# A fixed instruction order for the state-space stage of a hybrid decoder layer, with decays prepared in mid-step, the causal select in GpSimd's order, and the decay product last in a step

## The chip, the cores and the metric

The kernel runs on one core of a Trainium2 chip. The metric is the device time of one execution in microseconds (us); lower is better. The core has five engines with a queue of instructions each, which run in the order of the queue and wait for each other through semaphores: TensorE (PE, matrix products and transposes; PEld is its weight load), VectorE (DVE), ScalarE (ACT), GpSimd (POOL) and SyncE (SP). Transfers between DRAM and the core's memory are issued by SP and ACT. Matrix products are accumulated in eight PSUM banks of 128 x 512 float32.

## The reference, cut to what matters

One layer of a hybrid block on a sequence of 1024 tokens and width 1024, all in float32. Two branches read the same modulated input: a chunked gMLP (y_a) and a Mamba-2 state-space branch (y_b); a gate merges them and a last projection follows. The part that is changed here is the state-space scan and the norm behind it: 8 groups of 4 heads of 64 columns, a state of 128, chunks of 128 tokens. `segsum_exp` gives exp(a_cs[i] - a_cs[j]) where i >= j, and 0 elsewhere.

```python
def ssd_scan(x, dt, a, bmat, cmat):
    xd = (x * dt[..., None]).reshape(b, nc, q, g, r, p)
    a_cs = jnp.cumsum(adt, axis=-1)
    decay = segsum_exp(adt)
    cb = jnp.einsum('bclgn,bcsgn->bcgls', cc, bc)
    y_diag = jnp.einsum('bcgls,bcgrls,bcsgrp->bclgrp', cb, decay, xd)
    decay_to_end = jnp.exp(a_cs[..., -1:] - a_cs)
    chunk_states = jnp.einsum('bcsgn,bcgrs,bcsgrp->bcgrpn', bc, decay_to_end, xd)
    ...
    def step(state, inp):
        cs, cd = inp
        return state * cd[..., None, None] + cs, state
    ...
    y_off = jnp.einsum('bclgn,bcgrpn,bcgrl->bclgrp', cc, prev_states, jnp.exp(a_cs))
    return (y_diag + y_off)
...
y_b = y_b + xh * d_skip[:, None]
yz = (y_b * silu(ssm_z)).reshape(b, s, SSM_GROUPS, -1)
y_b = rms_norm(yz, ssm_norm_w.reshape(SSM_GROUPS, -1)).reshape(b, s, SSM_D_INNER)
merged = sigmoid(g_a) * (y_a @ w_proj_a) + sigmoid(g_b) * (y_b @ w_proj_b)
```

## The kernel before

**Stages.** The input is normed and transposed and the first products run (to about 70 us); `v_block` makes the v columns of the input projection by a seven-product scheme (p1 to p7) on halves of the matrix, each operand split into a high and a low part; pairs of columns of the other projections follow (`pair`), to about 920 us; then comes the state-space stage, then the projection of y_b, and the output product to the end.

**The state-space stage** is a list of 32 steps, `order`: two groups take turns, four steps each, and a step covers 256 tokens, two chunks. A step n consists of pieces that the loop at the end of the stage calls:

- `fetch`: SP loads the decay sums of a step, broadcast to all partitions (`dcy`, 512 KB), and the six rows of the step (`sl`, 768 KB: C, B, two of x, two of the gate z). There are five sets of these buffers, so a load into a set waits for the step five earlier.
- `decay`: ScalarE takes exp into `ea` (two instructions, L1067), GpSimd sets what is above the diagonal to -1e30 (`affine_select` on `dcy`, L1070), ScalarE takes eight exponentials of `dcy` in place (L1075).
- `prep`: TensorE makes C times B (`pc`) and transposes x (`px`) and B (the other half of `pc`); VectorE makes `xd` and `xe` from `px` (L1091) and multiplies `dcy` by `pc` (L1095); ScalarE copies B to `bn` (L1097).
- `front`: TensorE makes `yi` from `dcy` and `xd`, and the new states `sp` from `bn` and `xe`; the state is carried over each of the two chunks by a GpSimd product with the chunk's decay (L1123) and a VectorE sum with `sp` (L1125), or copied where there is none yet (L1121).
- `back`: TensorE makes `yn` from the states before the two chunks; `evacuate` adds the skip term to `yi` (L1151), multiplies `yn` by `ea` (`ym`, L1155), adds (L1156) and gates (L1157) on GpSimd; `post` stores every second step's rows (`yb_d`).
- Later pieces (`later(k, ...)`, run after k more pieces): `squares` (two ScalarE squares in place, L1176, and their sum on GpSimd, L1177), `post2` (a row sum by eight `pq` products, a VectorE instruction, L1186, and for each group a power of -0.5 on GpSimd, L1190), `post3` (a transpose, a copy and a store).

Between `front` and `back` of a step, `draw` issues four or five items of the gMLP projection (`proj_a`, tiles `pma`: two matmuls an item), so that TensorE has work while the state is summed. Beside it go the split of its weights (`wa_block`, L1280 and L1281) and the gate of its result (`tha`, L1382), 16 of each.

**What sets the order.** TensorE's instructions and SP's loads are pinned. `pin` (`keep_in_program_order`) puts an instruction behind the one that was traced before it on its engine, whether that one is pinned or not. All other instructions of VectorE, ScalarE and GpSimd are placed in their queue by a planner, which walks through the program by its own estimate of times and takes, of the instructions that it holds to be ready, the one of the highest priority: the earlier in the program, the higher, and those under `tc.high_priority()` (`front`, `back`, `prep`) first. Once placed, an engine's order is fixed. In the kernel before, nearly all of the stage's work on these three engines is left to the planner:

```python
for n in range(len(order)):
    if n > 1:
        step(n, "front")
        draw(6 if n == 2 else 4 + n % 2)
    step(n, "back")
    ...
    if n + 2 < len(order):
        step(n + 2, "prep")
    fetch(n + 6)
    decays(n + 4)
```

`decays(n + 4)` at the end of step n calls `decay` for step n+3.

## Time and profile before

| what | value |
|---|---|
| time, median of 3 runs (lowest to highest) | 1404.81 us (1404.6 to 1406.76) |
| the profiled execution's own time | 1402.83 us |
| its span, first to last instruction | 1401.1 us |
| mean granted TensorE clock | 0.996 |
| DMA traffic | 288.6 MB, mean 206 GB/s |

The page of the profile gives the busy time of each engine and its share of the span. Views of the trace follow in the prediction: busy time by stretches of the span (its columns are the stretch, its length, then for PE, PEld, DVE, ACT and POOL the busy us and the number of instructions, then the granted clock, the DMA share and GB/s); groups of instructions (line, engine, operation, out<-in, shapes, count, then busy us and mean ns of one, then the idle time of the engine before them with what ended it); waits (engine and line, what it waited for: us in total, times, longest); the timeline (start, length, engine, line, operation, in brackets the idle time before it); and the chain of waits that ended last.

### The profile page before, as it was taken

To read this page: it belongs to the slowest core of one execution; us is meant where nothing else is said; L and a number is where in the kernel's file an instruction comes from. 1 tells how busy PE (TensorE), PEld (TensorE's weight loads), DVE (VectorE), ACT (ScalarE), POOL (GpSimd) and SP (SyncE) were. 2 spreads that over 40 slices of the span, in tenths; PEclk is the share of its full clock that TensorE was granted. 3 is DMA by queue.
4 is the path that set the end of the run, shared out by engine and by line. 5 is a ranking of instruction groups with operands and counts; after the bars stand their busy time and mean duration, and the time that the engine had idled before them with its cause. 6 is when DMAs were issued, how large, how long until landed. Compare 5 with 4: busy or idle time off the path is not lost.

```text
span 1401.1 us, 20579 instructions
## 1 busy us (share of the span) xinstructions
PE 1369.7 (98%) x6971; PEld 1135.3 (81%) x6971; DVE 1055.3 (75%) x1815; ACT 804.7 (57%) x1496; POOL 217.8 (16%) x208
## 2 busy tenths in 40 slices
PE   8999999999999999999999999999999999999997
PEld 7678888888888888878888888888888788888786
DVE  4776776687777889888888795398777655859976
ACT  5754656666666566455675555677676623223453
POOL 0000000000000011211000110038878750000001
PEclk9999999999999999999999999999999999999999
DMA  8775433333434777777775774598887658878913
GB/s 263 197 237 147 120 121 120 105 123 118 135 105 128 225 219 230 220 238 226 215 220 148 241 214 134 179 354 319 279 267 278 220 185 280 319 254 313 378 44 120
DMA packets 277181, 288.62 MB, mean 206 GB/s; under 512 B 15788, under 2 KB 224084, under 8 KB 277076
## 3 DMA queue, kind: packets, MB, share of 16 engines
q1 hardware_dynamic: 182420, 203.76, 45.6%
q10 hardware_dynamic: 94656, 83.54, 18.1%
q8 instruction: 55, 0.90, 0.3%
q14 instruction: 50, 0.41, 0.1%
HBM read 199.79 MB, written 87.46 MB: 205 GB/s over the span
## 4 chain that ended last, share of the span: by engine, by line
PE 78%; DVE 7%; DMA 7%; ACT 3%; issue 3%; POOL 2%; SPq 1%; ACTq 0%; DVEq 0%; POOLq 0%
PE xuz L536 6%; PE xx L536 6%; PE xcb L536 6%; PE xz L536 5%; PE xg L536 5%; PE pma L81 4%; PE yx L536 3%; PE vx L918 3%; PE x L1552 3%; PE yuz L536 3%; PE yp L1552 3%; PE ycb L536 3%; PE yz L536 3%; PE ox L1745 2%; PE yg L536 2%
## 5 line engine op out<-in xcount | busy, mean ns | idle before, releaser
L759 POOL TENSOR_TENSOR wog<-wog,gb 128x256 f32<-128x256 f32 x16 | 21.5, 1362 | 624.0 <-DMA wog<-in_w_out_dram 602.9
L1075 ACT ACTIVATE dcy<-dcy,nacs 128x128 f32<-128x128 f32 x256 | 78.7, 388 | 17.2 <-POOL dcy L1070 16.1
L1070 POOL TENSOR_SCALAR_AFFINE_SELECT dcy<-dcy 128x1024 f32<-128x1024 f32 x32 | 35.0, 1094 | 135.4 <-DMA yl<-ya_d 88.7
L990 ACT ACTIVATE ac<-ac 128x1024 f32<-128x1024 f32 x32 | 33.9, 1060 | 25.8 <-DVE ac L988 22.6
L1067 ACT ACTIVATE ea<-dcy 64x512 f32<-64x512 f32 x64 | 40.0, 626 | 12.2 <-DMA dcy<-acs_d 11.8
L81 PE MATMUL pma<-yh,wah 128*128 128x512 f32 x128 | 43.8, 423 | 0.0
L81 PE MATMUL pma<-yh,wal 128*128 128x512 f32 x128 | 43.2, 419 | 0.0
L1490 DVE SCALAR_TENSOR_TENSOR yn<-yn,par,rb 128x512 f32<-128x512 f32 x32 | 23.9, 747 | 24.8 <-DMA yn<-yb_d 24.8
L1155 DVE TENSOR_TENSOR ym<-yn,ea 128x512 f32<-128x512 f32 (+1 forms) x32 | 19.9, 622 | 29.9 <-PE yn L81 29.7
L1095 DVE TENSOR_TENSOR dcy<-dcy,pc 128x1024 f32<-128x1024 f32 x32 | 38.9, 1217 | 3.8 <-PE pc L84 2.6
L1157 POOL TENSOR_TENSOR yz<-y,sl 128x512 f32<-128x512 f32 x32 | 41.4, 1294 | 1.1
L81 PE MATMUL pma<-yl,wah 128*128 128x512 f32 x128 | 40.3, 396 | 0.0
L1156 POOL TENSOR_TENSOR y<-y,ym 128x512 f32<-128x512 f32 (+1 forms) x32 | 36.6, 1143 | 14.5 <-DVE ym L1155 14.5
L81 PE MATMUL yi<-dcy,xd 128*64 128x128 f32 x512 | 35.9, 284 | 2.9 <-DVE st L1125 2.9
L81 PEld LDWEIGHTS yn<-sl,st 128*128 128x128 f32 x224 | 30.3, 190 | 8.8 <-issue 2.7
L81 PE MATMUL yn<-sl,st 128*128 128x128 f32 x224 | 31.4, 276 | 5.4 <-DVE st L1125 5.4
L81 PE MATMUL sp<-xe,bn 128*128 128x256 f32 x112 | 33.6, 418 | 2.9 <-DVE ssq L1186 1.7
L988 DVE SCALAR_TENSOR_TENSOR ac<-c2x,cwt,ac 128x1023 f32<-128x1023 f32 (+2 forms) x24 | 31.2, 1298 | 5.7 <-ACT ac L986 5.6
L1760 POOL TENSOR_TENSOR r<-r,fnw 128x512 f32<-128x512 f32 x2 | 2.5, 1296 | 208.2 <-ACT junk L1758 208.2
L988 DVE SCALAR_TENSOR_TENSOR ac<-c2cb,cwt,ac 128x1023 f32<-128x1023 f32 (+2 forms) x24 | 31.1, 1294 | 4.8 <-ACT ac L986 4.7
L1123 POOL TENSOR_TENSOR st<-st,cd 128x256 f32<-128x256 f32 x48 | 32.5, 677 | 11.2 <-PE yn L81 7.1
L952 ACT ACTIVATE vm<-vm,vr 128x128 f32<-128x128 f32 x64 | 25.8, 483 | 14.0 <-DMA vm<-v_d 13.5
(2903 smaller groups left out, 4421.7 us busy)
## 6 DMA issues: line engine op xcount, KB each, us to landing
sl<-s_d SPq DMA_DIRECT2D x32, 768.0 KB
s_d<-ac ACTq DMA_DIRECT2D x32, 512.0 KB
dcy<-acs_d SPq DMA_DIRECT2D x32, 512.0 KB
av<-in_w_in_dram SPq DMA_DIRECT2D x36, 256.0 KB
aw<-in_ada_w_dram SPq DMA_DIRECT2D x16, 512.0 KB
wbr<-in_w_proj_b_dram SPq DMA_DIRECT2D x64, 128.0 KB
wb_d<-wbb ACTq DMA_DIRECT2D x32, 256.0 KB
wb_d<-wbc ACTq DMA_DIRECT2D x32, 256.0 KB
```

What stands on the lines that cost most here:

```text
L81: pin(PE.matmul(acc, l, r, start=first, stop=last))
L536: pin(PE.matmul(ps, lw[:, k * P : (k + 1) * P], r[k], start=first and n + k == 0, stop=n == 2 and k == 3, skip_group_check=not first))
L918: pin(PE.matmul(ps[pn][j], l[:, js], r, start=nm in ("p1", "p5", "p2") and n + k == 0, stop=n == 2 and k == 3, skip_group_check=nm not in ...
L988: V.scalar_tensor_tensor(ac[:, s:], cc[:, : S - s], conv_wt[:, 3 - s, i : i + 1], ac[:, s:], op0=ALU.mult, op1=ALU.add)
L990: A.activation(ac, ac, AF.Silu)
L1067: A.activation(ea[hh * HD : (hh + 1) * HD], dcy.rearrange("p (j e) i l -> p e j (i l)", e=2)[hh * HD : (hh + 1) * HD, hh], AF.Exp)
L1070: G.affine_select(out=d8, in_=d8, compare_op=ALU.is_ge, fill=-1e30, base=0, pattern=[[0, 2 * HPG], [1, P]], channel_multiplier=-1)
L1075: A.activation(dcy[:, h, i, :], dcy[:, h, i, :], AF.Exp, bias=sub[:, i, h : h + 1])
L1095: V.tensor_tensor(d3, d3, pc[:, 0:256].unsqueeze(1).to_broadcast([P, HPG, 256]), op=ALU.mult)
L1156: G.tensor_add(y1[:, :, t0:], y1[:, :, t0:], m[:, :, t0:])
L1157: G.tensor_mul(yz, y1, sl[:, 4:6])
L1552: pin(PE.matmul(ps[j], a[:, v, js], r, start=first and n + k == 0, stop=n == 2 and k == KT - 1, skip_group_check=not first))
```

## The change

In the state-space stage:

- The VectorE and GpSimd instructions of `front`, `back`, `evacuate`, `post2` and the new `close` are pinned, and from the third step on those of `prep` and the select of `decay`.
- `decays` moves from the end of a step to its middle, ahead of the draws, and reaches a step less far: in step n it prepares step n+2.
- In `prep` the copy to `bn` goes from ScalarE to VectorE and comes first (two buffers in place of three), then `xd` and `xe`, and the product of `dcy` by `pc` is last.
- The state has fixed places for each of two groups: `mid`, after the first chunk of a step, and two ends. `front` adds `sp` to `mid`, which `close` of the group's step before has already multiplied, starts the product for the end, and adds the skip term to `yi`; `close`, after `back`, adds the second half of `sp` and multiplies for the next `mid`.
- `squares` comes 8 pieces later in place of 5.
- The power of -0.5 on GpSimd becomes a root by 11 pinned VectorE instructions.
- The low halves of the gMLP weights (`lows`) are made by pinned instructions between two draws.

Outside it: the first two units of `v_block` are interleaved so that two of its four banks come first, and the banks of the first sums after the stage (`yp`, `xp`) are allocated in another order.

```diff
@@ v_block
-            terms = list(enumerate(((bh, wh), (bl, wh), (bh, wl))))
-            for j, (n, (l, r)) in [(j, t) for t in terms for j in range(4)] if u < 2 else [(j, t) for j in range(4) for t in terms]:
+            at = [(u, n, j) for j in range(4) for n in range(3)]
+            if u == 0:
+                ends = [(0, 2, 0), (0, 2, 1)] + [(0, n, j) for j in (2, 3) for n in range(3)]
+                at = [(i, n, j) for i in range(2) for n in range(2) for j in range(2)] + ends
+            elif u == 1:
+                at = [(1, 2, 0), (1, 2, 1)] + [(1, n, j) for j in (2, 3) for n in range(3)]
...
@@ decay
+            keep = pin if s or g > 1 else lambda i: i
+            keep(G.affine_select(out=d8, in_=d8, compare_op=ALU.is_ge, fill=-1e30, base=0,
...
@@ prep
+            bn = p2x.tile([P, 256], F32, name=f"bn{nm}", tag="bn", bufs=2)
+            keep(V.tensor_copy(bn, pc[:, 256:512]))
             for v, f in (("xd", dthq), ("xe", dde)):
...
-            V.tensor_tensor(d3, d3, pc[:, 0:256].unsqueeze(1).to_broadcast([P, HPG, 256]), op=ALU.mult)
-            bn = p2x.tile([P, 256], F32, name=f"bn{nm}", tag="bn", bufs=3)
-            A.copy(bn, pc[:, 256:512])
+            keep(V.tensor_tensor(d3, d3, pc[:, 0:256].unsqueeze(1).to_broadcast([P, HPG, 256]), op=ALU.mult))
@@ front
+            mid, *ends = state(g % 2)
+            if s == 0:
+                pin(V.tensor_copy(mid, sp[:, 0:256]))
+            else:
+                pin(V.tensor_add(mid, mid, sp[:, 0:256]))
+            self.sts = [self.st, mid]
+            self.st = ends[s % 2]
+            if not last:
+                pin(G.tensor_mul(v3(self.st), v3(mid), fac(cd, g, s)[:, 1].unsqueeze(2).to_broadcast([P, HPG, HD])))
...
+            for j in range(2):
+                pin(V.scalar_tensor_tensor(y1[:, j], sl[:, 2 + j], dskt[:, 2 * g + j : 2 * g + j + 1],
+                                           yi[:, j * 256 : (j + 1) * 256], op0=ALU.mult, op1=ALU.add))
+        def close(self, s):
...
+            pin(V.tensor_add(self.st, self.st, self.sp[:, 256:512]))
+            pin(G.tensor_mul(v3(mid), v3(self.st), fac(cd, self.g, s + 1)[:, 0].unsqueeze(2).to_broadcast([P, HPG, HD])))
@@ evacuate
-            V.tensor_tensor(m[:, :, t0:], yn.rearrange("p (j l) -> p j l", j=2)[:, :, t0:], ea[:, :, t0:], op=ALU.mult)
-            G.tensor_add(y1[:, :, t0:], y1[:, :, t0:], m[:, :, t0:])
-            G.tensor_mul(yz, y1, sl[:, 4:6])
+            pin(V.tensor_tensor(m[:, :, t0:], yn.rearrange("p (j l) -> p j l", j=2)[:, :, t0:], ea[:, :, t0:], op=ALU.mult))
+            pin(G.tensor_add(y1[:, :, t0:], y1[:, :, t0:], m[:, :, t0:]))
+            pin(G.tensor_mul(yz, y1, sl[:, 4:6]))
@@ post, post2
-                later(5, self.squares, yz, [yz[:, j] for j in range(2)])
+                later(8, self.squares, yz, [yz[:, j] for j in range(2)])
...
-                G.tensor_tensor(ssq[:, c8], ssq[:, c8], nhalf, op=ALU.pow)
+                t, v = (ssq[:, n % NG * NCH : (n % NG + 1) * NCH] for n in (g, g + 2))
+                pin(V.tensor_scalar(sc.bitcast(I32), t.bitcast(I32), -0.5, float(0x5F3759DF), op0=ALU.mult, op1=ALU.add))
+                pin(V.tensor_scalar_mul(v, t, -0.5))
+                for n in range(3):
+                    pin(V.tensor_mul(t, sc, sc))
+                    pin(V.tensor_mul(t, t, v))
+                    pin(V.scalar_tensor_tensor(t if n == 2 else sc, t, 1.5, sc, op0=ALU.add, op1=ALU.mult))
@@ wa_block, proj_a
-            V.tensor_sub(wl, wr, f32(wh))
+            if dd == 0:
+                V.tensor_sub(wl, wr, f32(wh))
+            else:
+                lows.append((wl, wr, wh))
...
+                elif k in (3, 4) and lows:
+                    wl, wr, wh = lows.pop(0)
+                    pin(V.tensor_sub(wl, wr, f32(wh)))
@@ the stage's loop
             step(n, "front")
+            decays(n + 3)
             draw(6 if n == 2 else 4 + n % 2)
         step(n, "back")
+        with tc.high_priority():
+            groups[order[n][0]].close(order[n][1])
...
         fetch(n + 6)
-        decays(n + 4)
@@ after the stage
-                psy = banks("yp3", "y", 3)
-                psx = banks("x", "x")
-                psy += [psb.tile([P, 512], F32, name="yp33", tag="by3")]
+                first = {t: psb.tile([P, 512], F32, name=f"{t}p", tag=f"b{t}") for t in ('y0', 'y2', 'x0', 'x1', 'x2', 'x3', 'y3', 'y1')}
+                psx, psy = ([first[f"{v}{j}"] for j in range(4)] for v in "xy")
```

72 lines of the change are left out of this document (33 added, 39 removed).

## The prediction

> **What bounds the kernel now.** I read the busy shares first, then the busy time by stretches, then who waited for whom in the one stretch that is not full.
>
> ```profile
> PE 1369.7 (98%) x6971; PEld 1135.3 (81%) x6971; DVE 1055.3 (75%) x1815; ACT 804.7 (57%) x1496; POOL 217.8 (16%) x208
> ```
> ```profile
> core 0: us, PE busy (x) PEld busy (x) DVE busy (x) ACT busy (x) POOL busy (x), PEclk, DMA share, GB/s
> 80.00:940.00 860.00, 857.37 (x3889) 709.34 (x3888) 664.57 (x1103) 526.37 (x886) 46.67 (x37) 1.00 0.59 179
> 940.00:1140.00 200.00, 188.78 (x1441) 164.54 (x1440) 145.12 (x266) 129.39 (x337) 154.53 (x150) 0.98 0.75 259
> ```
> ```profile
> 1100.00:1104.00 4.00, 1.55 (x15) 1.55 (x16) 2.03 (x4) 3.98 (x14) 3.74 (x5) 0.72 0.13 52
> 1104.00:1108.00 4.00, 4.00 (x13) 2.93 (x12) 2.25 (x5) 3.04 (x9) 2.79 (x3) 0.50 0.30 68
> ```
>
> TensorE sets the time. From 80 to 940 us it is idle 2.6 us in 860. The state-space stage, 940 to 1140, has 200 - 188.8 = 11.2 us of idle, and behind one gap the granted clock is 0.50: the 1.6 + 4.0 us of work in those two rows, and a little after them, run at half speed, some 3 us lost. So 11.2 + 3 = 14.2 us are there to be won in this stage; more would need less TensorE work, and the change takes none away.
>
> ```profile
> L81 PE MATMUL yi<-dcy,xd x480: 272/273/473, 940.3 to 1139.1; 128*64 128x128 f32 x160
> ```
> ```profile
> 959.46 1.02 PE yi L81 x16
> 960.48 1.06 PE sp L81 x4
> 961.54 2.30 PE pma L81 x10
> 963.85 0.89 PE yn L81 x8
> 965.84 1.02 PE yi L81 x16
> ...
> 977.36 0.79 PE pq L81 x8
> ```
>
> The first row (one tile's instructions) holds 30 steps of 16 products between 940.3 and 1139.1, so 198/29 = 6.83 us a step. The others are one undisturbed step in the chain of waits (start, length, work): 6.38 us from yi to yi, the last 1.1 of it for pc and px; every second step has eight pq besides, 0.79. Taking idle and slow clock out of the mean gives (200 - 14.2)/200 x 6.83 = 6.34 us: what TensorE alone needs.
>
> ```profile
> PE yn L81 <- DVE st L1125: 5.4, 5, 2.1
> DVE st L1125 <- POOL st L1123: 13.3, 7, 5.8
> POOL dcy L1070 <- ACT ea L1067: 22.7, 15, 4.2
> ACT ea L1067 <- DMA dcy<-acs_d: 11.8, 7, 2.7
> ACT bn L1097 <- DVE dcy L1095: 20.9, 9, 6.2
> ```
> ```profile
> 1088.70 0.36 SPq L90 DMA_DIRECT2D dcy<-acs_d  x1
> ...
> 1098.93 1.27 ACT L1067 ACTIVATE ea<-dcy 64x512 f32<-64x512 f32 x2 [2.46 <-DMA dcy<-acs_d]
> ...
> 1100.26 1.09 POOL L1070 TENSOR_SCALAR_AFFINE_SELECT dcy<-dcy 128x1024 f32<-128x1024 f32 x1 [4.20 <-ACT ea L1067]
> 1101.32 0.61 POOL L1123 TENSOR_TENSOR st<-st,cd 128x256 f32<-128x256 f32 x1
> 1101.97 0.42 DVE L1125 TENSOR_TENSOR st<-st,sp 128x256 f32<-128x256 f32 x1 [5.76 <-POOL st L1123]
> 1102.45 0.91 PE L81 MATMUL yi<-dcy,xd 128*64 128x128 f32 x6 [2.87 <-DVE st L1125]
> ```
>
> The waits of 935 to 1145 (us in total, times, longest) read upwards as a chain, and the timeline shows its worst case. The transfer issued at 1088.70 lands 10.2 us later. It is the decay tile of step 29 (the thirtieth select of the trace), while TensorE is in step 25. The planner had put this select in GpSimd's queue ahead of the state product of step 25, which needs nothing of it. So a transfer that is urgent in three steps holds GpSimd for 4.20 us, VectorE for 5.76, TensorE for 2.87, and the half clock follows.
>
> **The change, part by part.** I write M for the state sum in the middle of a step, S for GpSimd's product behind it, K for the product after the closing sum C, W for the decay product out of yn, A and Z for GpSimd's two gating instructions, D for the product of decays.
>
> ```profile
> L1095 DVE TENSOR_TENSOR dcy<-dcy,pc 128x1024 f32<-128x1024 f32 x29 | 35.3, 1217 | 3.3 <-PE pc L84 2.1 <-issue 0.3 <-DMA sl<-s_d 0.2
> L1156 POOL TENSOR_TENSOR y<-y,ym 128x512 f32<-128x512 f32 (+1 forms) x30 | 34.6, 1152 | 12.1 <-DVE ym L1155 12.1
> L1157 POOL TENSOR_TENSOR yz<-y,sl 128x512 f32<-128x512 f32 x29 | 37.5, 1294 | 0.9
> L1123 POOL TENSOR_TENSOR st<-st,cd 128x256 f32<-128x256 f32 x44 | 30.0, 683 | 9.2 <-PE yn L81 6.5 <-DVE tha L1382 2.0 <-DVE st L1121 0.7
> L1091 DVE TENSOR_TENSOR xd<-px,dthq 128x512 f32<-128x512 f32 x29 | 19.8, 682 | 0.0
> L1125 DVE TENSOR_TENSOR st<-st,sp 128x256 f32<-128x256 f32 x45 | 18.4, 411 | 14.4 <-POOL st L1123 13.3 <-PE sp L81 1.1
> L1155 DVE TENSOR_TENSOR ym<-yn,ea 128x512 f32<-128x512 f32 (+1 forms) x29 | 18.4, 634 | 27.6 <-PE yn L81 27.3
> L1121 DVE COPY st<-sp 128x256 f32<-128x256 f32 x6 | 2.5, 418 | 0.9 <-PE sp L81 0.9
> L1177 POOL TENSOR_TENSOR yz<-yz 128x512 f32<-128x512 f32 x14 | 18.0, 1286 | 2.8 <-ACT yz L1176 2.8
> L1075 ACT ACTIVATE dcy<-dcy,nacs 128x128 f32<-128x128 f32 x216 | 66.4, 388 | 13.8 <-POOL dcy L1070 12.7 <-issue 0.6 <-DVE tha L1382 0.4
> ```
>
> Loads first. VectorE has 145.1/200 x 6.83 = 4.96 us of work in a step. It gains the bn copy, 0.42 by the copy of the same shape (L1121), and a root chain. GpSimd has 154.5/200 x 6.83 = 5.28 and loses the powers; ScalarE has 4.42 and loses the copy on which it waited 20.9 us. All stay below 6.34, so order decides, not load.
>
> The new order, laid on the undisturbed step with yi at 0: sp ends at 2.08, yn at 5.28. VectorE then does W 0.63, C 0.41, bn 0.42, xd and xe 0.68 each, D 1.22, together 4.04, to 9.32, and M to 9.73, which is 3.35 in the next step. TensorE wants M for the second half of yn, at 4.84 - with four draws in place of five 4.38. **Slack 1.0 to 1.5 us.** GpSimd: A behind W from 5.91 to 7.06, Z to 8.36, K to 9.04, that is 2.66 of the next step; S waits for M at 3.35 and ends at 4.03, select (1.09 in the timeline above) at 5.12, the eight exponentials (66.4/216 x 8 = 2.46) at 7.58. VectorE comes to D at 5.28 + 2.82 = 8.10, so there is half a microsecond more. Behind M in VectorE's queue stand the yi sums and W; behind S the select and A; PE waits for none of them sooner than counted.
>
> Decays now come at steps n to n+2: the select of step 29 moves from step 25 to step 27, two steps or 12.7 us later, more than the 10.2 us that its transfer took. The decays issue no transfer, and SP's loads keep their place in its queue; sl waits for Z, which comes at 7.1 as in good steps of before. That removes the chain above. The exponentials pay for it: they had more than a step in hand and now have 0.5 + 1.0. What comes late next is ScalarE's ea, which is not pinned: if the planner still floats it to the landing, it blocks the exponentials of two steps earlier. In full the seven waits cost each at most 2.7 - 1.6 = 1.1 us, 7.7 together; none at the other end; I take 2, since most are short.
>
> ```profile
> 154.96 0.17 DVE L110 TENSOR_TENSOR vr<-vr 128x8 f32<-128x8 f32 x1
> 155.16 0.17 DVE L111 SCALAR_TENSOR_TENSOR vr<-vr 128x8 f32<-128x8 f32 x1
> ```
>
> The power on GpSimd becomes 11 VectorE instructions of this kind, 0.20 from start to start: 2.2 us between D and M, in six steps of the loop. Each of these steps also has the eight pq products, 0.8 us of TensorE. The lag is 2.2 - 0.8 - 1.0 to 1.5, so 0 to 0.4; the ends are 0 and 6 x 2.2 = 13; I take 2 in all. Squares come three slots later; their sum on GpSimd (1.29, 14 times) fits the 0.8 us between select and A only in part: with the low halves of the weights pinned between draws, I take 3 us of lag, between 0 and 14 x 1.29 = 18. So of 14.2 us, 7 come back: **-7.2**.
>
> ```profile
> 1050.03 1.28 DVE L1281 TENSOR_TENSOR wal<-wa,wah 128x512 fp32r<-128x512 f32 x1
> 1050.73 1.05 POOL L1123 TENSOR_TENSOR st<-st,cd 128x256 f32<-128x256 f32 x1
> ```
>
> These two overlap other work of VectorE and GpSimd and last 1.28 and 1.05 us, where the product has 0.61 in the chain above. The Trainium skill ("SBUF — State Buffer", section "Who interferes with whom") says that a VectorE instruction with two SBUF inputs and a GpSimd instruction that reads SBUF block each other for a whole instruction. Nine instructions of each root chain are of that kind, so by the rule this part costs more than by the row of 0.20; the trace agrees with the rule.
>
> The two ends: the v products start with 10 matmuls that don't need banks 2 and 3, and the bank order before the projection changes.
>
> ```profile
> PE vx L918 <- ACT sg L473: 1.3, 1, 1.3
> PE x L1552 <- DVE tha L1382: 1.0, 1, 1.0
> ```
>
> Ten matmuls at 0.23 (10 draws' products in 2.30) cover 1.3, if the second unit's operands are there: -1.2, between -1.3 and 0. The other wait is for banks of the last draws, now given to sums that start later: -0.8, between -1.0 and 0. Costed at nothing: the states in fixed places and the y1 sums pulled into the front (the same instructions; they follow M in the 1 us or more that VectorE has before W), and the sp and pc banks, held longer now, sp to C at 6.32 and pc to D at 9.32. Five banks a step and eight in all cover that; a bank that is missed would hold the next yi until D ends, at most 9.32 - 6.38 = 2.9 us. **Sum: -7.2 - 1.2 - 0.8 = -9.2 us.** On the profiled execution (1402.83: span 1401.1 and 1.7 around it) that is 1393.6; the median of the runs is 2.0 above it, so 1395.6.
>
> **Rivals.** First, TensorE alone sets the stage: all 14.2 and both ends go, 1404.8 - 16.5 = 1388.3. For it: slack in every row above; against: the six root chains. Second, ea still blocks ScalarE: 7.7 in place of 2, with the 2 of the roots and the 3 of lag 12.7 of 14.2 come back; with the ends 1404.8 - 1.5 - 2.0 = 1401.3. For it: seven such waits before, and ea stays free to float; against it: ScalarE has 1.9 us free in a step. Third, the other sign: a closed loop becomes the bound. M, S, select, exponentials, D, M of the next step: 0.41 + 0.61 + 1.09 + 2.46 + 1.22 = 5.79, with four handovers of 0.05 (1101.93 to 1101.97 above) 6.0. Anything inside it that adds over 6.83 - 6.0 = 0.8 us in every step makes the stage slower than before. One ScalarE instruction (0.63) in front of the exponentials in each step and the squares' sum in half of them (0.64) give 7.27: 29 x (7.27 - 6.83) = +12.8, less 2 at the ends, 1415.6. Against it: these have room outside the loop. Fourth, the planner's order was about this one already and the waits only change names: 1404. Against it: the select two steps early. Fifth, the root chains meet GpSimd at their nine two-input steps. GpSimd stands still behind M once K has ended at 2.66 of the next step, so a chain meets at most the rest of K and one squares' sum: 6 x 1.29 = 7.7 more, 1403.3. Against it: the sums can fall elsewhere.
>
> By the rule of the Trainium skill named above, with GpSimd at work all the time, each of the nine steps could wait a whole instruction; no row here shows such a chain.
>
> **How the numbers follow.** Forecast 0.36, first rival 0.14, second 0.18, third 0.17, fourth 0.09, fifth 0.06, together 1. A measurement of this kernel tells about 0.2%, 2.8 us, from no change. Faster, below 1402.0: 0.36 + 0.14 + 0.13 of the second + 0.02 of the fifth = 0.65; within: 0.05 + 0.09 + 0.04 = 0.18; slower 0.17. The time is 1395.6, the forecast's own range 1391 to 1400. The range for 8 in 10 goes from the first rival, 1388, into the third, 1409.
>
> **What would show it.** Right: idle TensorE time of the stage under 8 us, no clock of 0.50 in it, no select waiting for ea by over 2 us, D last in a step; yi to yi 6.4 to 6.6. Wrong: TensorE waits for M or D in most steps (the loop), ScalarE's exponentials waiting behind ea for the transfer, GpSimd waiting for squares. A gap in steps with root chains over 1 us would put that price wrong. If the v products wait at their fifth matmul, the gain at that end is gone.

## The result, and the profile after

The changed kernel takes 1415.36 us (median of 7 runs, 1411.23 to 1418.42), the kernel before beside it on the same chip 1406.18 (7 runs): a ratio of 1.0061, with a 95% interval of 1.0042 to 1.008. It is slower by 0.6%. The forecast was 1395.6 with a range to 1409, so both the sign and the range were wrong. A second measurement of the same pair (the run `e15_after_again` below) gave 1.0081 (1.0056 to 1.0106). The profiled execution of the changed kernel took 1414.67 us, its span is 1412.9; line numbers from here on are those of the kernel that a view is of.

The page's engine line, and the busy time of the state-space stretch, which answers to the row of before (same columns):

```profile
PE 1374.9 (97%) x6971; PEld 1139.6 (81%) x6971; DVE 1089.0 (77%) x1935; ACT 796.0 (56%) x1464; POOL 208.7 (15%) x200
```
```profile
940.00:1140.00 200.00, 188.40 (x1402) 164.44 (x1402) 172.50 (x353) 121.19 (x308) 143.52 (x143) 0.97 0.74 255
```

TensorE was to lose most of its 11.2 us of idle time in the state-space stage; it has 11.6. VectorE went from 145 us and 266 instructions to 172 and 353, over twice what the bn copies account for.

Fixed stretches hide that the steps themselves have shifted. So I cut each trace where the 16 yi products that begin a step start, with a second profile of each kernel beside the first (`e12_before_again`, `e15_after_again`):

| us | start to first yi | steps 1 and 2 | third yi to last (29 steps) | last yi to the end |
|---|---|---|---|---|
| before | 921.7 | 18.5 | 198.0 | 262.8 |
| before, second profile | 925.5 | 18.5 | 198.7 | 263.4 |
| changed | 920.9 | 23.4 | 201.0 | 267.6 |
| changed, second profile | 924.3 | 23.0 | 203.3 | 267.0 |

The first column varies by 4 us between two profiles of the same kernel and tells nothing. The other three each tell: +4.7 in the first two steps, +3.8 in the stage, +4.2 behind it, by the means. Three different places lose, and each has its own rows.

**The stage.** First who waited for whom in it (us in total, times, longest):

```profile
ACT yz L1190 <- DMA yb_d<-yz: 21.2, 16, 3.3
ACT ea L1073 <- DMA dcy<-acs_d: 16.6, 10, 3.3
POOL dcy L1077 <- ACT ea L1073: 16.0, 14, 2.8
PE yn L81 <- DVE st L1127: 10.3, 4, 4.2
POOL st L1131 <- DVE st L1127: 9.1, 5, 5.1
```

Before, the closing and middle sums waited for GpSimd's product (13.3 us). Now GpSimd and TensorE wait for the middle sum M (L1127), TensorE four times, 10.3 us. The timeline around the longest of the four, VectorE first, then GpSimd, then TensorE (`...` stands for rows left out):

```profile
1016.66 1.27 DVE L1203 TENSOR_SCALAR sc<-ssq 128x8 int32<-128x8 int32 x1
1017.85 0.16 DVE L1204 TENSOR_SCALAR ssq<-ssq 128x8 f32<-128x8 f32 x1
1018.04 1.25 DVE L1206 TENSOR_TENSOR ssq<-sc 128x8 f32<-128x8 f32 x1
1019.33 0.54 DVE L1207 TENSOR_TENSOR ssq<-ssq 128x8 f32<-128x8 f32 x1
1019.90 0.17 DVE L1208 SCALAR_TENSOR_TENSOR sc<-ssq,sc 128x8 f32<-128x8 f32 x1
...
1020.90 1.09 DVE L1207 TENSOR_TENSOR ssq<-ssq 128x8 f32<-128x8 f32 x1
1022.02 1.21 DVE L1208 SCALAR_TENSOR_TENSOR ssq<-ssq,sc 128x8 f32<-128x8 f32 x1
1023.15 0.41 DVE L1127 TENSOR_TENSOR st<-st,sp 128x256 f32<-128x256 f32 x1
...
1016.61 1.29 POOL L1170 TENSOR_TENSOR y<-y,ym 128x512 f32<-128x512 f32 x1
1017.98 1.29 POOL L1171 TENSOR_TENSOR yz<-y,sl 128x512 f32<-128x512 f32 x1
1019.23 0.61 POOL L1145 TENSOR_TENSOR st<-st,cd 128x256 f32<-128x256 f32 x1
1020.88 1.09 POOL L1077 TENSOR_SCALAR_AFFINE_SELECT dcy<-dcy 128x1024 f32<-128x1024 f32 x1 [1.04 <-ACT ea L1073]
1021.94 1.27 POOL L1191 TENSOR_TENSOR yz<-yz 128x512 f32<-128x512 f32 x1
...
1023.71 0.68 PE L81 MATMUL yn<-sl,st 128*128 128x128 f32 x4 [4.17 <-DVE st L1127]
```

The eleven instructions of a root chain last 0.17 us each where GpSimd stands still (1019.90 to 1020.90) and, five of them, as long as GpSimd's instruction where it works: these five end within 0.05 us of A, Z, K, the select and the squares' sum. The chain takes 6.57 us, where the forecast had 2.2, and M stands behind it.

This is the longest of the six chains of the loop. The first one, 7 us earlier, has less than 0.4 us of GpSimd's work beside it (VectorE, then TensorE):

```profile
1009.58 0.21 DVE L1203 TENSOR_SCALAR sc<-ssq 128x8 int32<-128x8 int32 x1
...
1011.51 0.17 DVE L1208 SCALAR_TENSOR_TENSOR ssq<-ssq,sc 128x8 f32<-128x8 f32 x1
1011.60 0.41 DVE L1127 TENSOR_TENSOR st<-st,sp 128x256 f32<-128x256 f32 x1
...
1011.43 1.41 PE L81 MATMUL yn<-sl,st 128*128 128x128 f32 x8
```

It takes 2.1 us, as forecast, and the eight yn products run through with a wait of 0.12 us. By the same trace the six chains last 2.1, 6.6, 4.2, 6.6, 2.1 and 4.6 us (in the fourth, a gMLP sum stands between its instructions for 3.1 of them); the steps of the two short ones are 7.1 us from yi to yi, those of the other four 9.8 to 11.4. Summed over the 29 steps of the third column, these six steps take 56.0 and 55.4 us in the two profiles of the changed kernel, against 41.3 and 45.3 for the same steps before; the other 23 take 145.0 and 147.8 against 156.7 and 153.4. So the new order wins some 9 us where no chain stands and the chains' steps lose 12.

**The first two steps, and behind the stage.** The timeline where the operands of the third step are prepared, VectorE and then TensorE; and then of the place where the norms of group 6 are transposed:

```profile
936.93 1.41 DVE L1406 SCALAR_TENSOR_TENSOR tha<-tha,pma 128x512 f32<-128x512 f32 x2 [2.48 <-DMA tha<-th_d]
...
938.39 0.44 PE L84 MATMUL px<-ident,sl 128*128 128x128 f32 x2 [2.78 <-DVE tha L1406]
...
1176.29 0.75 DVE L1523 SCALAR_TENSOR_TENSOR yn<-yn,par,rb 128x512 f32<-128x512 f32 x1 [2.84 <-DMA yn<-yb_d]
...
1177.56 0.15 DVE L1199 TENSOR_SCALAR ssq<-y0p 128x4 f32<-128x4 f32 x1
...
1179.64 0.75 DVE L1523 SCALAR_TENSOR_TENSOR yn<-yn,par,rb 128x512 f32<-128x512 f32 x1 [1.44 <-DMA yn<-yb_d]
...
1182.70 0.16 DVE L1208 SCALAR_TENSOR_TENSOR ssq<-ssq,sc 128x8 f32<-128x8 f32 x1
...
1182.92 0.38 PE L84 MATMUL y2p<-ident,ssq 128*8 128x128 f32 x1 [4.77 <-DVE ssq L1208]
```

In the first, px wants a PSUM bank that the gMLP projection's sum (`tha`; the expectations call this projection the last one) gives back, and that sum waits on VectorE for a load. In the second, the scale of the norms and the chain stand between instructions that wait for loads of yb_d; TensorE reaches the transpose and stops. Behind four of the five gaps of over 2 us in this profile the granted clock is 0.50, for 3.4 or 6.8 us.

Of the rows that were to show the forecast right, two came: D is last in a step, and where no chain falls yi to yi is 6.4 us in the mean, as forecast, though spread from 5.5 to 7.2 (the last step, 4.5, aside). The idle time stayed, half clock came more often, and one select still waited 2.8 us for ea. The four gaps of 1.51 to 4.17 us behind M are those over 1 us that "would put that price wrong".

### The profile page after: what moved, and what is told of

Same layout as the page of the kernel before. It is cut to its first block, busy times and chain, and to the rows that moved or that the text cites. A ratio compares the mean times of both kernels' runs of the same rounds, so it can differ in the third digit from the quotient of the medians.

```text
span 1412.9 us, 20668 instructions
## 1 busy us (share of the span) xinstructions
PE 1374.9 (97%) x6971; PEld 1139.6 (81%) x6971; DVE 1089.0 (77%) x1935; ACT 796.0 (56%) x1464; POOL 208.7 (15%) x200
## 3 DMA queue, kind: packets, MB, share of 16 engines
q1 hardware_dynamic: 182420, 203.76, 45.3%
## 4 chain that ended last, share of the span: by engine, by line
PE 80%; DMA 9%; DVE 6%; ACT 2%; issue 1%; SPq 1%; ACTq 0%; POOL 0%; DVEq 0%
PE xuz L536 6%; PE xx L536 6%; PE xcb L536 5%; PE xz L536 5%; PE xg L536 4%; PE pma L81 4%; PE vx L923 3%; PE yx L536 3%; PE yp L1585 3%; PE yuz L536 3%; PE ycb L536 3%; PE ox L1777 2%; PE yg L536 2%; PE yz L536 2%; PE oy L1777 2%; PE yi L81 2%
## 5 line engine op out<-in xcount | busy, mean ns | idle before, releaser
L81 PE MATMUL yn<-sl,st 128*128 128x128 f32 x224 | 31.9, 279 | 10.8 <-DVE st L1127 10.3
L958 ACT ACTIVATE vm<-vm,vr 128x128 f32<-128x128 f32 x64 | 25.8, 483 | 14.7 <-DMA vm<-v_d 14.2
L994 DVE SCALAR_TENSOR_TENSOR ac<-c1cb,cwt,ac 128x1023 f32<-128x1023 f32 (+2 forms) x24 | 31.6, 1319 | 1.3 <-ACT ac L992 1.3
```

The costliest lines, as they stand in the source:

```text
L81: pin(PE.matmul(acc, l, r, start=first, stop=last))
L994: V.scalar_tensor_tensor(ac[:, s:], cc[:, : S - s], conv_wt[:, 3 - s, i : i + 1], ac[:, s:], op0=ALU.mult, op1=ALU.add)
```

## The experiments

Runs in one group were timed on one chip, beside runs of the kernel before on that chip, and the ratios are to those; the groups (e1 to e4, e5 to e8, e9 to e12, e13 to e15, e16 and e17, e18) lie on several chips, so ratios compare, and medians only within a group. The parts are those of the table above. They are of one execution each, and not always a typical one: e17's was the fastest of its nine (1394.76 us), e4's and e5's the slowest of theirs (1421.54 and 1415.71). e1 and e5 have the same code from the third step on and differ in the stage by 5.7 us, so a difference of a few us between two single profiles shows little.

| run | median us (runs) | ratio, 95% interval | steps 1, 2 | stage | behind |
|---|---|---|---|---|---|
| e1_pow_back | 1408.47 (12) | 1.0029, 1.0006 to 1.0051 | 22.9 | 191.8 | 265.6 |
| e2_root_on_before | 1416.03 (7) | 1.0074, 1.0048 to 1.0101 | 18.5 | 204.4 | 264.4 |
| e3_pow_late | 1418.44 (6) | 1.0092, 1.006 to 1.0123 | 21.1 | 200.0 | 266.1 |
| e4_root_psum | 1417.27 (8) | 1.0082, 1.0054 to 1.0111 | 21.0 | 199.1 | 269.4 |
| e5_tha_later | 1410.28 (12) | 1.0038, 1.0021 to 1.0056 | 21.3 | 197.5 | 267.7 |
| e6_tail_later | 1408.29 (12) | 1.0019, 0.9998 to 1.004 | 21.3 | 195.4 | 264.6 |
| e7_decays_end | 1406.94 (12) | 1.0017, 0.9996 to 1.0038 | 23.0 | 194.0 | 262.0 |
| e8_chain_behind_M | 1414.49 (7) | 1.0061, 1.0037 to 1.0085 | 23.4 | 196.7 | 268.1 |
| e9_squares_later | 1408.77 (12) | 1.0028, 1.0006 to 1.0049 | 23.2 | 195.8 | 263.3 |
| e10_more_filler | 1408.39 (12) | 1.0029, 1.0012 to 1.0046 | 22.4 | 193.3 | 266.1 |
| e11_filler_end | 1408.96 (12) | 1.0033, 1.0018 to 1.0049 | 22.4 | 193.0 | 265.8 |
| e12_before_again | 1405.25 (12) | 1.0004, 0.9981 to 1.0026 | 18.5 | 198.7 | 263.4 |
| e13_head | 1404.19 (12) | 0.999, 0.9974 to 1.0005 | 19.3 | 194.4 | 261.9 |
| e14_banks_alone | 1403.46 (12) | 0.9988, 0.9971 to 1.0005 | 18.5 | 197.5 | 262.7 |
| e15_after_again | 1417.06 (6) | 1.0081, 1.0056 to 1.0106 | 23.0 | 203.3 | 267.0 |
| e16_sum_behind_S | 1399.38 (12) | 0.9964, 0.9944 to 0.9984 | 19.3 | 192.7 | 262.8 |
| e17_and_mid_decays | 1399.16 (9) | 0.9954, 0.9935 to 0.9973 | 19.3 | 191.3 | 261.8 |
| e18_chain_alone | 1407.37 (12) | 1.0007, 0.9989 to 1.0025 | 19.5 | 199.2 | 263.5 |

### The root chain: four runs with it and without it

`e1_pow_back`, in `post2` of the changed kernel:

```diff
-                t, v = (ssq[:, n % NG * NCH : (n % NG + 1) * NCH] for n in (g, g + 2))
-                pin(V.tensor_scalar(sc.bitcast(I32), t.bitcast(I32), -0.5, float(0x5F3759DF), op0=ALU.mult, op1=ALU.add))
...
+                c8 = slice(g * NCH, (g + 1) * NCH)
+                G.tensor_tensor(ssq[:, c8], ssq[:, c8], nhalf, op=ALU.pow)
```

> The changed kernel with one thing undone: the inverse root of the row norms is again one pow on GpSimd in all eight groups, in place of the eleven-instruction chain on VectorE. Theory A (the root chain costs what the change lost: gaps of 4.17, 2.30, 1.51, 2.32, 0.48 and 4.77 us behind it and three to four half-clock windows, some 24 us together): the six gaps are gone or under 1 us each, no clock of 0.50 in the state-space stage, time about 1391 (1387 to 1398), some 23 us below the changed kernel, and below the kernel before. Rival B (the pinned order closes the loop of state, selection, exponentials and decay product, and the chains only show where it is slow anyway): the gaps stay at the same steps behind other releasers, time 1408 to 1418. Rival C (half of it is the wait on the load of the last projection's operand at 938 us and its half clock): about 1402.

`e2_root_on_before` is the same edit the other way round, in the kernel before.

> The kernel before with one thing added: the eleven-instruction root chain on VectorE in place of the pow on GpSimd, pinned at the same place in the order of its own engine. Theory A (the chain is dear by itself): slower than before by 8 to 20 us, 1414 to 1426, with gaps of TensorE over 1 us in the steps with root chains, and single chain instructions of over 1 us that each end with an instruction of GpSimd. Rival B (the chain is dear only in the pinned order of the changed kernel): within 4 us of before, 1403 to 1410. My prediction's price, 2.2 us of VectorE over all of them at two places, would give 1408.

`e3_pow_late` takes the pow for `g >= NG - 2` alone.

> The changed kernel with the pow on GpSimd back for groups 6 and 7 alone, whose norms fall into the projection stage; the chain stays for groups 0 to 5. Theory A: the gap of 4.77 us at 1183 us and its half-clock window of 6.8 us go, the other five gaps stay: 5 to 9 us below the changed kernel, 1406 to 1410. Rival (at that place the transpose waits for the norms' matmul and the scale behind it, and not for the chain): the gap keeps more than half of its length, time within 3 us of the changed kernel.

`e4_root_psum` keeps the chain and puts one operand of each product into the bank of `pq`:

```diff
-                    pin(V.tensor_mul(t, sc, sc))
+                t, w = pq[:, 8:16], pq[:, 16:24]
...
+                    pin(V.tensor_copy(w, sc))
+                    pin(V.tensor_mul(t, sc, w))
```

> The changed kernel with the root chain at the same place but three copies longer (fourteen instructions), so that none of its instructions reads two operands of SBUF: one operand of each lies in PSUM. Theory A1 (a small VectorE instruction with two SBUF inputs stands still while GpSimd is in an instruction, so the eleven instructions wait for five or six whole GpSimd instructions): the chain takes 3 us or less, from 6.6, no instruction of it above 0.5 us, and the three gaps of the loop fall to under 1.5 us each: time 1395 to 1403. Rival A2 (the chain is long since each instruction waits for the result of the one before it and VectorE is full, wherever the operands lie): the chain stays at 6 us or more, time 1414 to 1420. Rival A3 (GpSimd holds up every VectorE instruction that touches SBUF at all, one input or two): as A2, with the copies stretched too.

The pow wins back 0.3 to 0.5% of the 0.6 to 0.8, not all: e1 is still slower than before (1.0029, interval above 1). Its stage is at 191.8, 6.5 us under before, and those of four more kernels with the pow (e5, e6, e7, e9) at 194.0 to 197.5, against 199.1 to 203.3 for the changed kernel, e3 and e4; but the two other places stay long. So theory A is right about the stage and wrong about the rest: its sum had counted all six gaps and their half clock as the chain's, and its time of 1391 did not come. e2 agrees from the other side: 0.7% for the chain alone, and the stage 6 us longer. e3 went as its rival had it: the transposes wait 0.91 and 3.70 us for the pow as they did for the chain, since what is late there is the scale ahead of both. VectorE, GpSimd and TensorE in e1 show it:

```profile
1176.47 0.75 DVE L1518 SCALAR_TENSOR_TENSOR yn<-yn,par,rb 128x512 f32<-128x512 f32 x1 [2.01 <-DMA yn<-yb_d]
1177.14 0.15 DVE L1199 TENSOR_SCALAR ssq<-y1p 128x4 f32<-128x4 f32 x1
...
1177.37 1.65 POOL L1203 TENSOR_TENSOR ssq<-ssq,nhalf 128x8 f32<-128x8 f32 x1 [4.99 <-DVE ssq L1199]
...
1179.07 0.27 PE L84 MATMUL y3p<-ident,ssq 128*8 128x128 f32 x1 [3.60 <-POOL ssq L1203]
```

e4 splits the chain's price in two. Its timeline on VectorE, where the first chain of the loop is from 1018.21 to 1020.88 (the second, at 1025.85, has 0.82 in its first instruction and ends 3.3 us after):

```profile
1018.21 0.22 DVE L1204 TENSOR_SCALAR sc<-ssq 128x8 int32<-128x8 int32 x1
...
1018.47 0.17 DVE L1207 COPY pq<-sc 128x8 f32<-128x8 f32 x1
1018.67 0.17 DVE L1208 TENSOR_TENSOR pq<-sc,pq 128x8 f32<-128x8 f32 x1
...
1020.71 0.17 DVE L1210 SCALAR_TENSOR_TENSOR ssq<-pq,sc 128x8 f32<-128x8 f32 x1
1020.80 0.41 DVE L1127 TENSOR_TENSOR st<-st,sp 128x256 f32<-128x256 f32 x1
```

Without a second SBUF operand no product waits for GpSimd any more, so mechanism A1 is shown. The six steps with a chain take 48.0 us, 7 to 8 less than in the changed kernel, and their gaps at yn are 0.69 to 1.69 us. But the forecast of the time failed: the ratio is that of the changed kernel. In this profile the other 23 steps take 151.0 us, 3 to 6 more, and the transpose behind the stage waits 6.47 us in place of 4.77. The shorter chain is cheaper where it stands; why the whole is not faster stays open.

### Behind M instead, and the chain alone

`e8_chain_behind_M` calls the same chain one item later, `later(1, self.root)`, so that it follows M and the y sums:

> The changed kernel with its root chain one item later in the loop's groups: behind M and the y sums of the next step and ahead of its W, with the same eleven instructions. Theory F (a chain costs what it delays M by, since the products of the next step, yn, wait for M in TensorE's order, and it is cheap behind M): the three gaps of the loop behind chains fall to under 1 us each, the stage from the third step's yi to the last's 192 to 195 us from 201.0, time 1406 to 1410. Rival G (W, the closing sum and K stand behind the chain now, and the next M behind these, so that the same 4 to 7 us come one half step later): 199 to 203 us, time 1413 to 1418.

```profile
1030.89 0.70 PE L81 MATMUL sp<-xe,bn 128*128 128x256 f32 x2 [4.21 <-DVE ym L1169]
```

The stage is 5 us shorter than the changed kernel's (between what F and G have), but the longest gap is now at sp, behind W, and the time is the changed kernel's, as rival G says. Part of what the stage wins is lost behind it, in a gap of 4.95 us at 1168.63 for a gMLP sum that the changed kernel does not have. In the whole time, the chain is as dear behind M as ahead of it.

`e18_chain_alone` came last, and prices the chain where the other stalls are mended: the fastest kernel of the study (below) with the change's chain in place of the pow.

> The kernel of the run before it, the fastest so far (0.9954), with the change's root chain on VectorE, at the change's place between D and M, in place of the pow on GpSimd. It prices the chain where no other stall stands beside it. By my forecast's term, 2 us over all: ratio 0.996 to 0.997. By the pairs so far (e1 against the changed kernel 0.3 to 0.5%, e2 against before 0.7%): 4 to 11 us, ratio 0.999 to 1.003, gaps of over 1 us at yn behind the chains, and single instructions of the chain over 1 us.

Against the pow it costs 0.53% by the two ratios (1.0007 and 0.9954), some 7.4 us; their intervals leave 4 to 11. The stage of each, cut from the third yi to the last, e17 and then e18, and the eight us behind the longest gap of e18 (3.81):

```profile
939.90:1131.20 191.30, 185.10 (x1421) 162.05 (x1420) 154.07 (x293) 120.65 (x308) 152.23 (x148) 0.99 0.78 267
```
```profile
939.30:1138.50 199.20, 188.10 (x1422) 164.57 (x1421) 173.29 (x358) 121.32 (x308) 143.49 (x142) 0.97 0.76 256
1012.00:1016.00 4.00, 3.92 (x19) 3.95 (x19) 2.72 (x6) 2.20 (x4) 0.61 (x1) 0.50 1.02 412
1016.00:1020.00 4.00, 4.00 (x24) 3.48 (x24) 3.93 (x7) 2.80 (x10) 3.60 (x4) 0.50 0.34 128
```

The idle time goes from 191.3 - 185.1 = 6.2 to 11.1 us, and the same products are busy 3.0 us longer, at half clock: 4.9 + 3.0 = 7.9.

### The first two steps

`e5_tha_later`, on e1: the first two sums of the gMLP projection are made behind `close` of the second step.

```diff
+            if dd: finish()
+            else: first_tha.append(finish)
...
+        if n == 1:
+            first_tha.pop()()
```

> The kernel of the run with the pow put back, with one more thing moved: the first two sums of the last projection (L1406 in the changed kernel), which wait for the load of th_d, stand on VectorE behind the decay product of the third step instead of ahead of the two W of the first two steps. Theory D (TensorE's gap of 2.59 us at 941.84 us and the half-clock window of 3.4 us behind it come from that wait, since W, the closing sum and the PSUM readers of the next step are queued behind it): the gap goes, from the second step's yi to the third's 11.5 to 12.5 us from 16.2, time 1402 to 1406, some 4 us less. Rival (something else is late there, the transposes' bank or the load of the stream): another releaser, the same 16 us, time 1407 to 1411.

`e13_head`, on e7 below:

```diff
     for n in range(2):
         step(n, "front")
+        with tc.high_priority():
+            groups[order[n][0]].close(order[n][1])
         draw(10)
```

> The kernel of the run e7_decays_end with the closing sum of the first two steps right behind their y sums, as in the kernel before, instead of behind their yn. Theory I (the first steps are 3 to 5 us longer since the update products sp of both steps keep their PSUM banks until the closing sum, while the first two pairs of the last projection still hold four: with yn and the transposes more than eight banks are wanted, and yn and the transposes wait for whichever is freed last, L1406, L1144 or L1101): the gaps of 1.33, 0.51 and 1.58 us at 939 to 943 us go, from the first yi to the third 18.3 to 19.5 us from 23.0, time 1401 to 1405. Rival (the waits belong to the order of W and the operand copies on VectorE): 22 us or more, time 1406 to 1409.

In e5 the wait for the load is gone and 1.6 us of the 4.4 with it. The rest has new releasers, C and then xe:

```profile
942.53 0.44 PE L84 MATMUL px<-ident,sl 128*128 128x128 f32 x2 [0.51 <-DVE st L1144]
945.11 0.68 PE L81 MATMUL yn<-sl,st 128*128 128x128 f32 x4 [1.59 <-DVE xe L1101]
```

Whatever gives a bank back last is waited for. e13 gives the banks of sp back early, and the two steps fall from 23.0 to 19.3, as theory I said; no gap there is over 0.28 us. This was 0.27% of the time (1.0017 to 0.999, with intervals that overlap).

`e10_more_filler` (on e9 below) put `draw(2 + 4 * n)` for `n < 2` in place of `draw(4)` at `n == 1`, and `e11_filler_end` the decays of e10 at the end of a step:

> The kernel of the run before it with four pairs of products of the last projection more between the sums and the operand preparation of the first two steps (2 and 6 in place of 0 and 4), taken from the ones left behind the loop. If the 2.8 us that the first steps are longer than in the kernel before (14.67 against 11.88 us from the second yi to the third, with gaps of 0.29, 0.51 and 1.58 us) are only waits in the order: these gaps fall under 1 us in all; from the second yi to the third 14 to 15 us with 1.8 us more work in it, time 1 to 2 us under the run before. Rival: the loop's end lacks them then, no change.

> The kernel of the run before it with the decays at the end of a step again, as in the kernel before the change. By the run e7_decays_end (1.0017 against 1.0019) no difference: within 2 us of the run before. If the waits of the selection are the next bound once the store's wait is gone: 3 to 5 us slower.

More work between did not hide the wait for banks: 22.4 us, and the products taken from behind the stage were missing there (266.1, with 3.91 us at 1163.63 for a gMLP sum). The rival of e10 is what happened; e11 moved nothing.

### Behind the stage, and the place of the decays

`e6_tail_later`, on e5, and `e7_decays_end`, on e6:

```diff
-        if nm == "p1" and k in (3, 4):
-            groups[NG - 5 + k].post3()
+        if nm == "p1" and k in (4, 5):
+            groups[NG - 6 + k].post3()
```
```diff
             step(n, "front")
-            decays(n + 3)
...
         fetch(n + 6)
+        decays(n + 4)
```

> The kernel of the run before it, and the two transposes of the last groups' norms (post3 of groups 6 and 7) one unit of the output projection later in TensorE's order. Theory E (the gap of 3.60 us at 1179.07 us arises because the scale of the norms stands on VectorE one load of yb_d later than in the kernel before, and the transpose waits in TensorE's order for it): the gap falls under 1.5 us and its half-clock window goes, from the last step's yi to the end 263 us (261 to 264.5) from 265.6, time 1397 to 1403. Rival (a later transpose brings the norms of groups 6 and 7 too late for their rows, and the wait comes back at the products that need them): as long as before, 1402 to 1406.

> The kernel of the run before it with the exponentials and selection of later steps prepared at the end of a step again (four steps ahead) instead of in its middle. If the place of the decays is what won the state-space stage (198.0 us before, 191.8 with the pow back, from the third step's yi to the last's): 4 to 7 us slower than the run before it, selection waits on the exponentials between 1 and 2.5 us in most steps. If the hand-written order of the sums, W, A, Z and K won it: within 2 us of the run before it.

e6 takes 3.1 us from the part behind the stage by these two profiles, 1.0 by that of e1, which has e5's order there; the kernels with e6's order that follow have 261.8 to 263.5 (e10 and e11 apart, which lack products there). Of e5's gaps of 1.57 and 3.34 us one of 2.61 stays, and the time is not the 1397 to 1403 expected, so E is right in direction and not in full. In e7 the decays made no difference to the time, where the forecast had most of the stage's gain hang on them; nor did they between e10 and e11 (above) or e16 and e17 (below).

### GpSimd's order

`e9_squares_later` (on e6) has `later(11, self.squares, ...)` and `later(18, self.post2, ...)` for 8 and 17.

> The kernel of the run e6_tail_later with the squares of a finished pair of steps taken three tasks (one step) later (11 instead of 8; their sum over partitions at 18 instead of 17). Theory H (the squares overwrite yz in place, so ScalarE waits for the store of yz to land, 19.6 us in 15 waits in that run, and their sum stands on GpSimd ahead of the state product of the next step, so that the closing sum, the operand copies and the update product sp come late: gap of 4.68 us at 1128.75 us): the waits on the store fall under 5 us, that gap under 1 us, the stage from the third step's yi to the last's 189 to 192 us from 195.4, time 1401 to 1404. Rival (the store lands late whenever it is asked for, or GpSimd is late for another reason, the selection's wait on the exponentials): the gap stays over 2 us, time 1406 to 1410.

Theory H fell: the waits on the store are 18.9 us in 13, and the norms' products wait in place of sp (1.48 and 2.99 us). But it left the question where the sum of the squares stands. The timeline of e13 around its first step of 11 us, ScalarE, GpSimd, VectorE, TensorE:

```profile
1013.40 0.63 ACT L1190 ACTIVATE yz<-yz 128x512 f32<-128x512 f32 x1 [3.35 <-DMA yb_d<-yz]
...
1015.06 1.26 POOL L1191 TENSOR_TENSOR yz<-yz 128x512 f32<-128x512 f32 x1 [3.72 <-ACT yz L1190]
1016.28 1.64 POOL L1203 TENSOR_TENSOR ssq<-ssq,nhalf 128x8 f32<-128x8 f32 x1
1017.89 0.61 POOL L1131 TENSOR_TENSOR st<-st,cd 128x256 f32<-128x256 f32 x1
...
1018.53 0.42 DVE L1144 TENSOR_TENSOR st<-st,sp 128x256 f32<-128x256 f32 x1 [5.28 <-POOL st L1131]
...
1020.63 0.70 PE L81 MATMUL yn<-sl,st 128*128 128x128 f32 x4 [1.85 <-DVE xe L1101]
```

The square waits for the store of what it overwrites, the sum for the square, S for both and the pow, and C, the operand copies and yn for S. `e16_sum_behind_S` moves two instructions, and `e17_and_mid_decays` adds `decays(n + 3)` in the middle of a step again:

```diff
-            G.tensor_add(sq[0], sq[0], sq[1])
+            later(1, lambda: pin(G.tensor_add(sq[0], sq[0], sq[1])))
...
+                root = lambda: pin(G.tensor_tensor(ssq[:, c8], ssq[:, c8], nhalf, op=ALU.pow))
+                later(1, root) if g < NG - 2 else root()
```

> The kernel of the run e13_head with two instructions of GpSimd moved one item later: the sum of the two squares (L1191), which waits for ScalarE and through it for the store of yz, and the pow, both now behind the state product S of the next step and ahead of its A, instead of ahead of S. Theory H (the two steps of 11.1 and 11.3 us that are left, with gaps of 1.85 and 0.83 us at 1020 to 1022 and 3.20 at 1127 and 10 us of half clock behind them, come from S waiting behind these two): the closing sum's waits on S fall under 1.5 us each, both steps to 7 to 8 us, the stage from the third step's yi to the last's 187 to 190 us from 194.4, time 1398 to 1401, faster than both kernels. Rival (A, Z and K come late instead, and with them M of the next step): the same two steps or their neighbours keep their gaps, time 1403 to 1406.

> The kernel of the run before it with the decays prepared from the middle of a step, as in the change. If nothing but the store and GpSimd's order limited the stage: within 2 us of the run before. If the waits of the selection on the exponentials are what is left: 2 to 4 us faster.

Both are faster than both kernels: 0.9964 and 0.9954. In e16 the closing sum's longest wait for S is 2.9 us, and the two steps of 11.1 and 11.3 us are 6.4 and 6.5; the stage shortens only by 1.7 us, as others now take 8 to 9.6. e17 and e16 can't be told apart in time (1399.16 and 1399.38).

The longest step that is left, 12.5 us in e17, can be read from the chain of waits that ended last:

```profile
1044.04 6.14 DMA dcy<-acs_d
...
1051.61 1.09 POOL dcy L1077
1052.70 0.59 POOL st L1131
...
1056.87 1.03 PE yn L81 x4
```

A transfer, the select (which had waited 4.53 us for ea), then S right behind it, and through C, the operand copies and D the sum M that TensorE waits for. It is the chain that the change set out to remove. The longest step of e16 (9.6 us) begins the same way, with a transfer of 5.52 us.

### The other two parts alone

`e14_banks_alone` is the kernel before with the change's `v_block` and bank order:

> The kernel before with only two parts of the change: the order of the v products' first two operands, and the order in which the output projection takes its banks. My prediction: 1.2 and 0.8 us less, by the gaps of 1.30 us at 72.61 us and 1.34 at 1328.78 us, 0.99 at 1158.93 us, all gone; ratio 0.998 to 0.999. Rival: the load behind them is the wait, and it comes back at the next product.

The gap of 1.30 us at 72.61 is gone. The two others are not: 1.07 us at 1159.88, for the same gMLP sum, and 1.24 at 1328.87, a wait that the bank order doesn't touch. The ratio of 0.9988 has 1 inside its interval. The last two runs are the ones in the first table:

> The kernel before, profiled on this chip. If the profiled parts of the kernel before are its own and not one run's: first yi at 920 to 924 us, from the third step's yi to the last's 196 to 200 us, from the last yi to the end 261 to 264 us, and the time 1400 to 1408. If the time before the first yi is a chip's or a run's matter (921 to 930 us in the runs so far, with the same code), it lies anywhere in that.

> The changed kernel, profiled and timed on this chip. First yi at 921 to 930 us, as with the other kernels of the same first part; from the first yi to the third 21 to 24 us, from there to the last 198 to 203, from there to the end 266 to 270; ratio 1.004 to 1.008. If the parts differ by more than 3 us from the first profile, differences of that size between single profiles say nothing.

In these two the first yi came at 925.5 us before and at 924.3 in the changed kernel, so its lateness in the other runs is not the change's.

## Why the prediction was wrong

- **The root chain** is the largest term that failed. "I take 2 in all", between 0 and 13: it is 7.9 us by the profiles of e18 and e17, 4 to 11 by their ratios. What failed in it is the duration. It came from a row of a stage in which GpSimd was idle (0.17 us); the chain's own neighbours were in the fifth rival, with the argument that GpSimd "stands still behind M once K has ended". It does not: A, Z and K of the step before, the select and the squares' sum all ran beside the longest chain. The other half, a slack of 1.0 to 1.5 us ahead of M, was about right: in the changed kernel's steps without a chain the second half of yn starts 0.8 to 2.2 us after M has ended (first profile), and two chains of 2.1 us made TensorE wait 0.12 us. The chain alone does not turn the sign: without it the kernel is still slower than before (e1), and with the other stalls mended it only takes the whole gain away (e18).
- **Banks, "costed at nothing".** "Five banks a step and eight in all cover that" left out the four that the gMLP projection's sums hold in the first two steps. The price named for a missed bank was 2.9 us; 3.7 were won back by e13.
- **Behind the stage**, -0.8 was counted and +4.2 came. That late chains and scales would stand among VectorE's waits for loads was not looked at; the transposes one unit later (e6) give back 1 to 3. The gap that the bank order was to close is still open in e14, where that order is changed alone; in the changed kernel it is gone.
- **GpSimd's squares.** "I take 3 of lag" for their sum was near: e16 wins 1.7 us in the stage and 0.26% of the time (0.999 to 0.9964). But the cause was the wait for a store, not room in the queue; and e16 moves the pow with the sum, so the share of each is not known.
- **The select.** The chain read off before (transfer, exponentials, select, state product) was the right one, but "I take 2, since most are short" left too little for it. e17 still has these waits:

```profile
POOL dcy L1077 <- ACT ea L1073: 27.6, 15, 4.5
ACT ea L1073 <- DMA dcy<-acs_d: 13.8, 8, 4.6
```

  The select waits more than before (22.7), and in the longest step of e17 S stands right behind it, as it did before. Preparing the decays in mid-step did not cure it (e7, e17 against e16). Why most of these waits no longer reach TensorE is not shown.
- **v_block**: the gap is gone as forecast; 1.3 us is below what the time before the first yi varies by.

That the size of the gain comes out near in the end is luck. With the three stalls mended the stage is 191.3 us (e17, its fastest execution; e16 has 192.7) against 198.35, and that kernel is 0.46% or 6.5 us faster than before, where the sum had -9.2. But e17 has neither the chain nor the late squares' sum, and by the forecast's own terms such a kernel had 14.2 - 2 = 12.2 us to win in the stage, not 7. The third rival's 1415.6 hit the time, not the mechanism: its loop adds "in every step", and steps without a chain take 5.5 to 7.2 us.

What is not settled: why e4, whose chains are shorter, is not faster than the changed kernel, and why the select's waits hold TensorE in some steps of e16 and e17 and not in others.

## What to carry to other kernels

Take the duration of a small instruction from a row with the same engines busy beside it, not from wherever the same shape occurs; here the same eleven instructions took 2.1 us with GpSimd almost idle and 6.6 with it at work. Before anything is put into an in-order queue, ask what stands behind it and whether it waits for a store or a load: two instructions moved by one place (the squares' sum and the pow behind S) gave as much back as the whole repair of the first two steps. When a tile is given back later, count the banks at the fullest moment, which is the start of the stage and not its steady step.

## What the runs showed of the hardware

A VectorE instruction of eight columns can last as long as the GpSimd instruction that it meets, 1.25 us in place of 0.17. The Trainium skill ("SBUF — State Buffer", section "Who interferes with whom") states this for instructions with two SBUF inputs, and for `tensor_scalar` in its two-port modes; the trace agrees on the first (L1206 to L1208), and e4, with one operand in PSUM, from the other side. L1203, a `tensor_scalar` with one input, lasted 1.27 us beside GpSimd and 0.21 without it; whether it ran in such a mode no run here shows.

Behind gaps of 2 to 5 us in TensorE's work the granted clock was mostly 0.50, for 3.4, 6.8 or (e18) 10.2 us; behind others of that length (2.32 us at 1138.51 in the changed kernel) it was not. e18 has 10.2 us of it in the stage and e17 3.4; the same products are busy 3.0 us longer in e18, near half of the difference.
